# A hybrid S5, retention and SwiGLU layer on one core: S5 parameter scratch in the table memory, padded C cleared at the start, key products and norm steps placed later or earlier

## The chip, the cores and the metric

The kernel runs on one core of a Trainium2 chip. The metric is the device time of one execution in microseconds (us); lower is better. The core has a matrix engine (PE, with its weight loads shown apart as PEld), a vector engine (DVE), a scalar engine (ACT), a general engine (POOL), and SP, which here only issues DMAs. The profile's times count from the start of its span.

## The reference

The reference computes one layer for 256 prompt tokens and 8 sequences of 8 decode tokens, 320 tokens in all, at width 2048, in fp32. Cut to what matters:

```
h = rms_norm(x, norm_mix)
u, q, k, v, g = split(h @ w_in)                 # widths 1024 each
s5 = s5_mixer(u, state, lam, log_step, b, c, d, w_glu, b_glu)
o  = retention_chunked(rotary(q), rotary(k) * 128**-0.5, v, state)   # 8 heads of 128
ret = silu(g) * group_norm(o) * ret_gn_w
x = x + concat([s5, ret]) @ w_out
gate, up = split(rms_norm(x, norm_ffn) @ w_ffn_in)
x = x + (silu(gate) * up) @ w_ffn_out
y = rms_norm(x, norm_final)

# s5_mixer: 64 groups of 16 channels, 64 complex states each
lam_bar = exp(lam * dt);  b_bar = ((lam_bar - 1) / lam) * b
xs = associative_scan(a * x + b_bar @ u)        # over the tokens
y  = Re(c @ xs) + d * u;  gelu(y) * sigmoid(gelu(y) @ w_glu + b_glu)

# retention, per head and chunk of 128 tokens
scores = (q @ k.T) * mask
o = scores @ v + (q @ r) * q_decay
r = r * chunk_decay + (k * k_decay).T @ v
```

The outputs are y for all tokens, and the new S5 and retention states.

## The kernel before, in words

**Matrix products.** Each weight is read in fp32 and split into two parts, hi (a cast on ACT, L130) and lo (a difference on DVE, L131); the activations are split in the same way. A 128 x 128 piece of a weight then goes through PE in three products with all 320 tokens (L141 to L143): hi by xhi, hi by xlo, lo by xhi. These three are called a block below. The function gemm runs blocks one after the other; the projections' result is ps_p.

**What runs between the blocks.** Everything else (the S5 part and the retention heads) is written as generators. After each block gemm adds 0.4 to a counter, clk.now, and run_due starts every generator whose time has come; a generator that yields a number sleeps for that much of the counter. The numbers are in the table DL (L799). They set the order on PE and on POOL, which follow the program's order. SP's order stands in the program, too, while a scheduler orders ACT and DVE by priorities; instructions under tc.high_priority go ahead.

**S5 parameters.** Once at the start, some 100 small DVE operations turn lam and log_step into the powers of lam_bar and their products (s5_step, L359, and s5_params, L365): rr, lp, ff, gp, the cosines and sines ecs, and lx0, the start states by lam_bar^4. Their intermediates are cut out of a piece of scratch by T(), and newscr(i) sets which piece (L319). It is the memory of cls_[i], named cl in the profile: cl is the padded C matrix of an S5 chunk, 1280 columns on 128 partitions, two of them, used by chunks in turn. s5_step begins in cls_[0], the exponentials of the parameters go to cls_[1] (newscr(1)), and lx0 is worked out in cls_[0] again. When that is done, POOL clears both cl (L451), so that the chunks find zeros where C is padded.

**S5 tables.** From ecs POOL builds tab, the cosines and sines of every chunk's 64 steps: 32 columns in four groups of 8 (s5_tables, L460). Group 0 is built at once, the groups 1 to 3 later, about 68 counter units apart (L415). Chunk c's scan on DVE reads four of the columns (s5_chunk, L500), so a group serves two chunks. A chunk has transposes (pt), small products (pk_, pb), the scan, and its output product py, into which cl goes.

**Retention heads.** Three generators for each of the 8 heads:
- head_k (L642): the key transposes pst; ACT scales them into kd and copies the decode keys into kv; the scores pss by three products; DVE multiplies the scores by the mask mk into sm (two parts) and smp (decode).
- head_v (L663): the value transposes pst2 (a pst in the profile too); ACT scales them into vT; DL["o"] later the output po = sm by vT and smp by vT, then the state product psr. DVE takes statistics of po (bn_stats, bn_aggr: st, mv). POOL makes scale and shift of them in eight small steps (L696 to L703: mv, gy), ACT normalises into `on` (L706), and DL["c"] later PE transposes `on` back into pn.
- pst, pss, pst2, pt, pk_, psr, pn all share one PSUM tag, misc, with two buffers.

**Second norm.** Late in the output projection ffn_norm (L1029) sums the squares, acc, on PE into ps_r, DVE takes the reciprocal root in some 12 small steps (ms, ry, rt), and PE spreads it over the partitions (ps_r2). DL["n2"] and DL["n2b"] place the two PE steps.

Of the kernel before, what the change touches and what calls it, by code (L numbers as in the profile page):

```python
# [44 lines left out]
def hybrid_kernel(ctx, tc, xT, w_in, w_out, w_glu, w_fi, w_fo, vecs, s5p, bc, x0,  # L45
# [3 lines left out]
    pe, act, dve, pool, sp = nc.tensor, nc.scalar, nc.vector, nc.gpsimd, nc.sync  # L49
# [20 lines left out]
    o = 0  # L70
# [104 lines left out]
    def tt(out, a, b, op):  # L175
        dve.tensor_tensor(out, a, b, op)
        return out
# [118 lines left out]
    tab = s5.tile([P, 2, NPAIR, NCP], F32, name="tab", tag="tab", bufs=1)  # L296
# [14 lines left out]
    d0s = [s5.tile([P, 2, 4, NCP], F32, name=f"d0{i}") for i in range(2)]  # L311
    xps = [s5.tile([P, 2, 4, NC], F32, name=f"xp{i}") for i in range(2)]
    cls_ = [s5.tile([P, 2, 4, CH + 1, 32], F32, name=f"cl{i}") for i in range(2)]
    bl0 = s5.tile([P, 2, 2, 2, 32], F32, name="bl0")
    kbd = s5.tile([P, CH, P], F32, name="kbd")
    for t_ in (*d0s, *xps, bl0, kbd):
        pool.memset(t_, 0.0)
    scr = [None, 0]

    def newscr(i):  # L320
        scr[0] = cls_[i].rearrange("p r j t h -> p (r j t h)")
        scr[1] = 0

    def T(shape):
# [34 lines left out]
    def s5_params(dt_):  # L359

        ang = T(she)
        tt(ang[:, 0], prm[:, 1], dt_, MUL)
        ts(ang[:, 1], ang[:, 0], 8.0, MUL)
        ts(ang[:, 2], ang[:, 0], 64.0, MUL)
        nn = ts(T(she), ang, float(1 / np.pi), MUL, MAGIC, ADD)  # L365
        ts(nn, nn, MAGIC, SUB)
        for part in PI_PARTS:
            stt(ang, nn, -part, ang, MUL, ADD)
        par = ts(T(she), nn, 0.5, MUL, MAGIC, ADD)
        ts(par, par, MAGIC, SUB)  # L370
        stt(par, nn, 0.5, par, MUL, SUB)
        tt(par, par, par, MUL)
        ts(par, par, -8.0, MUL, 1.0, ADD)
        a2 = tt(T(she), ang, ang, MUL)
        ec, es = ecs[:, 0:NE], ecs[:, NE:]
        q = T(she)
        ts(q, a2, 1.0 / factorial(13), MUL, -1.0 / factorial(11), ADD)
        for kk in (9, 7, 5, 3, 1):
            tt(q, q, a2, MUL)
            ts(q, q, (1.0 if (kk // 2) % 2 == 0 else -1.0) / factorial(kk), ADD)  # L380
        tt(q, q, ang, MUL)
        tt(es[:, 0::3], q, par, MUL)
        q = T(she)
        ts(q, a2, -1.0 / factorial(14), MUL, 1.0 / factorial(12), ADD)
        for kk in (10, 8, 6, 4, 2, 0):
            tt(q, q, a2, MUL)
            ts(q, q, (1.0 if (kk // 2) % 2 == 0 else -1.0) / factorial(kk), ADD)
        tt(ec[:, 0::3], q, par, MUL)
        for l in range(2):
            n = (NE - 1 - l + 2) // 3  # L390
            c_, s_ = ec[:, l::3][:, :n], es[:, l::3][:, :n]
            u1, u2 = T([P, n, NPAIR]), T([P, n, NPAIR])
            tt(u1, c_, c_, MUL)
            tt(u2, s_, s_, MUL)
            tt(ec[:, l + 1::3][:, :n], u1, u2, SUB)
            stt(es[:, l + 1::3][:, :n], c_, 2.0, s_, MUL, MUL)
        for g in range(4):
            if g == 0:
                for _ in s5_tables(ec, es, g):
                    pass  # L400
            else:
                spawn(s5_tables(ec, es, g), max(0.0, T0 - 40.0 + 2 * PER * g - clk.now))
        newscr(1)
        lr = tt(T(sh), prm[:, 0], dt_, MUL)
        vexp(rr, lr, sh)
        tt(lp[:, 0, 0], rr, ec[:, 0], MUL)
        tt(lp[:, 1, 0], rr, es[:, 0], MUL)
        den = tt(T(sh), prm[:, 0], prm[:, 0], MUL)
        d2 = tt(T(sh), prm[:, 1], prm[:, 1], MUL)
        tt(den, den, d2, ADD)  # L410
        rden = T(sh)
        dve.reciprocal(rden, den)
        nr = ts(T(sh), lp[:, 0, 0], -1.0, ADD)
        t1 = tt(T(sh), nr, prm[:, 0], MUL)
        t2 = tt(T(sh), lp[:, 1, 0], prm[:, 1], MUL)  # L415
        tt(t1, t1, t2, ADD)
        tt(ff[:, 0], t1, rden, MUL)
        t3 = tt(T(sh), lp[:, 1, 0], prm[:, 0], MUL)
        t4 = tt(T(sh), nr, prm[:, 1], MUL)
        tt(t3, t3, t4, SUB)  # L420
        tt(ff[:, 1], t3, rden, MUL)
        r2 = tt(T(sh), rr, rr, MUL)
        tt(r4, r2, r2, MUL)

        def cmul(o, a, b, shape):

            u1, u2 = T(shape), T(shape)
            tt(u1, a[0], b[0], MUL)
            tt(u2, a[1], b[1], MUL)
            tt(o[0], u1, u2, SUB)  # L430
            tt(u1, a[0], b[1], MUL)
            tt(u2, a[1], b[0], MUL)
            tt(o[1], u1, u2, ADD)

        def ri(t, i):
            return (t[:, 0, i], t[:, 1, i])

        def rep_(t, n):
            return tuple(t[:, q].unsqueeze(1).to_broadcast([P, n, NPAIR]) for q in range(2))

        cmul(ri(lp, 1), ri(lp, 0), ri(lp, 0), sh)
        cmul(ri(lp, slice(2, 4)), rep_(lp[:, :, 1], 2), ri(lp, slice(0, 2)), [P, 2, NPAIR])
        cmul(ri(gp, slice(0, 3)), rep_(ff, 3), ri(lp, slice(0, 3)), [P, 3, NPAIR])
        newscr(0)

        def b8(a):
            return a.unsqueeze(2).to_broadcast(shx)

        cmul((lx0[:, 0], lx0[:, 1]), (x0t[:, 0], x0t[:, 1]), (b8(lp[:, 0, 3]), b8(lp[:, 1, 3])), shx)
        for t_ in cls_:  # L450
            pool.memset(t_, 0.0)  # L451
        for q in range(2):
            for d in range(2):
                o = lpc[:, :, q, 4 * d:4 * d + 4]
                act.mul(o, lp[:, q].rearrange("p e (c j) -> p c j e", j=4), -1.0 if d > q else 1.0)
                o = gpc[:, :, q, 4 * d:4 * d + 4]
                act.copy(o[:, :, :, 0], ff[:, q].rearrange("p (c j) -> p c j", j=4))
                act.copy(o[:, :, :, 1:], gp[:, q].rearrange("p e (c j) -> p c j e", j=4))
# [41 lines left out]
    def s5_chunk(c):  # L500
# [21 lines left out]
        for w_, pc in ((0, gpc), (1, lpc)):  # L522
# [14 lines left out]
            for g in range(2):  # L537
                ps_, hs = slice(64 * g, 64 * g + 64), slice(16 * g, 16 * g + 16)
                if w_:
                    tt(cl[ps_, 0, :, 1:, hs], m1[ps_, 0:4], m2[ps_, 4:8], SUB)  # L540
                    tt(cl[ps_, 1, :, 1:, hs], m1[ps_, 4:8], m2[ps_, 0:4], SUB)
        yield DL["b1"] + (4.0 if c == 0 else 0.0)
        bst = s5.tile([P, 8, P], F32, name="bst", tag="bst", bufs=1)[:, 0:4]
# [3 lines left out]
        act.copy(bst, pt.rearrange("p (i s) -> p i s", s=P))  # L547
        yield DL["k1"]
        pk_ = misc("pk_")
# [5 lines left out]
        for j in range(4):  # L555
            r = slice(32 * j, 32 * j + 32)
            act.copy(kbd[r, :, r], pk_[r, 0:P].rearrange("p (d h) -> p d h", h=32))
        yield DL["b2"]
        pb = ps_b.tile([P, 2, 512], F32, name="pb", tag="pb", bufs=1)
# [32 lines left out]
        for r in range(2):  # L592
            act.copy(xs[:, r, :, :, 0], x0t[:, r, js])
            act.copy(xs[:, r, :, :, 1], ends[:, 0, r, js])
        yield DL["scan"]
        py = ps_y.tile([P, 512], F32, name="py", tag="y", bufs=1)
# [43 lines left out]
        return a  # L640

    def head_k(h, q_, qg, k_, R):  # L642
        yield DL["k"] + (2.5 if h == 0 else 0.0)
        pst = misc("pst")
        for i, s in enumerate(STARTS):
            tr(pst[:, P * i:P * i + P], k_[:, s:s + P])
        kd = mp.tile([P, 2, P], F32, name="kd", tag="kd", bufs=1)
        for i in range(2):
            act.mul(kd[:, i], pst[:, P * i:P * i + P], kdc[:, h, i:i + 1])
        act.mul(kv[64:128, h], pst[64:128, 2 * P:3 * P], kdc[64:128, h, 2:3])  # L650
        pss = misc("pss")
        mm(0.43, pss[:, 0:256], k_[:, 0:P], q_[:, 0:256], start=True, stop=True)
        mm(0.22, pss[:, 256:384], k_[:, P:256], q_[:, P:256], start=True, stop=True)
        mm(0.22, pss[:, 384:448], k_[:, 192:320], q_[:, 256:320], start=True, stop=True)
        sm = mp.tile([P, 384], F32, name="sm", tag="sm", bufs=1)
        mk = R["mk"]
        tt(sm[:, 0:256], pss[:, 0:256], mk[:, 0:NP], MUL)
        tt(sm[:, 256:384], pss[:, 256:384], mk[:, 0:P], MUL)
        tt(smp[64:128, :, 0:NS], pss[64:128, 384:448].rearrange("p (b t) -> p b t", t=NS),
           mk[64:128, NP:320].rearrange("p (b t) -> p b t", t=NS), MUL)  # L660
        R["kd"], R["sm"] = kd, sm

    def head_v(h, v_, qg, rt, R):  # L663
        yield DL["v"]
        pst2 = misc("pst2")
        for i, s in enumerate(STARTS):
            tr(pst2[:, P * i:P * i + P], v_[:, s:s + P])
# [27 lines left out]
        m_, t_, y_, w_ = mv[:, 0], mv[:, 1], y[:, 0], y[:, 1]  # L695
# [93 lines left out]
    def do_g(h):  # L789
        ps = proj(11 + 4 * h)  # L790
        sg = mp.tile([P, N], F32, name="sg", tag="sg", bufs=2)
        with tc.high_priority(offset=EVAC):
# [3 lines left out]
        spawn(sg_mul(h, sg))  # L796
        run_due()

    DL = dict(b1=14.2, k1=2.2, b2=4.6, scan=15.6, x=2.2, k=5.5, v=6.1,  # L799
              o=2.2, u=6.0, c=10.0, n2=3.0, n2b=2.4, nm=7.8)  # L800
    T0, PER = 52.6, 34.0


# [6 lines left out]
    with tc.high_priority(offset=100000):  # L810
        with tc.manual_schedule(engines={mybir.EngineType.SP}):
            act.dma_start(vec, vecs)
            k0 = 0
            for b, k1 in enumerate((2, 4, 8, 12, 16)):
                c, q = k0 // 4, slice(k0 % 8, (k1 - 1) % 8 + 1)
# [109 lines left out]
        tt(u2, src[1], m[0], MUL)  # L925
        tt(out[:, 1], u1, u2, ADD)

    newscr(1)
    finp = s5.tile([P, 2, NPAIR], F32, name="finp", tag="m0", bufs=1)
    fins = s5.tile([P, 2, NPAIR, NB], F32, name="fins", tag="m1", bufs=1)  # L930
    fin(finp.unsqueeze(3), [endp[:, r].unsqueeze(2) for r in range(2)],
# [301 lines left out]
```

## Time and profile before

| | |
|---|---|
| median of three runs | 1486.57 us (1485.52 to 1486.83) |
| the profiled execution | 1487.18 us |
| its span, first to last instruction | 1485.4 us |
| mean granted TensorE clock | 0.991 |
| PE busy from 57 to 92 us (35 us) | 25.83 us, granted clock 0.85 |
| PE busy from 272 to 283 us (11 us) | 6.86 us, granted clock 0.69 |
| PE busy from 545 to 1160 us (615 us) | 615.00 us, granted clock 1.00 |
| HBM read, written | 219.35 MB, 8.95 MB |

A row of a timeline gives the start, the length of the busy stretch, the engine, the line of the kernel, the operation with what it writes and reads, and, in brackets, how long the engine was idle before it and what released it. A row of the waits gives the engine, the tile and line that waited, the engine, tile and line that ended the wait, and then the sum, the number and the longest of such waits. The granted clock is the share of full speed that the throttle gave PE; the tenths in the profile's overview show it at 8 of 10 in two of forty slices and at 9 (90% or more) in the others.

### The profile page before, as it was taken

Reading aid. Unit: us, or ns where it says so; the run is one execution under the profiler, and the core shown is the slowest. Engines: PE = TensorE matmul, PEld = TensorE weight load, DVE = VectorE, ACT = ScalarE, POOL = GpSimd, SP = SyncE. Lnnn points to the kernel's source line nnn. Section 1 sums busy time; section 2 is a strip of 40 time slices with the busy share of each in tenths; the row PEclk is TensorE's granted clock in tenths of the full one; section 3 lists DMA queues with packets and bytes.
Section 4 is the critical chain, followed back from the end, with each engine's and each line's share of the span. In section 5 each row is a group of like instructions: output and inputs, shape, how many; then the busy total and the mean of one; then the engine's idle time right before and its main releaser. Section 6 shows DMA issues by size and latency. Waiting matters only on the chain.

```text
span 1485.4 us, 26187 instructions
## 1 busy us (share of the span) xinstructions
PE 1450.8 (98%) x10654; PEld 1430.6 (96%) x10654; DVE 849.8 (57%) x1411; ACT 616.5 (42%) x988; POOL 104.1 (7%) x228
## 2 busy tenths in 40 slices
PE   8979999899999999999999999999999999999997
PEld 7979999899999999999999999999999999999996
DVE  8967667567846765665445444444444454444454
ACT  6545555554525543333333333333333333333352
POOL 1333501412000000000000000000000000000001
PEclk9989999999999999999999999999999999999998
DMA  7534444344644466665444345444444544445443
GB/s 268 160 112 146 139 148 147 111 137 127 207 146 152 146 213 191 214 216 185 155 145 155 119 154 168 157 150 148 139 137 152 172 153 147 152 123 152 148 150 110
DMA packets 82312, 232.10 MB, mean 156 GB/s; under 512 B 17808, under 2 KB 30224, under 8 KB 82192
## 3 DMA queue, kind: packets, MB, share of 16 engines
q1 hardware_dynamic: 82048, 230.39, 48.9%
q8 instruction: 84, 1.38, 0.4%
q14 instruction: 36, 0.29, 0.1%
q10 hardware_dynamic: 144, 0.04, 0.0%
HBM read 219.35 MB, written 8.95 MB: 154 GB/s over the span
## 4 chain that ended last, share of the span: by engine, by line
PE 68%; DVE 1%; DMA 0%; ACT 0%; issue 0%; DVEq 0%; SPq 0%
PE ps_fo L142 7%; PE ps_fu L143 7%; PE ps_fo L143 7%; PE ps_fu L141 7%; PE ps_fu L142 7%; PE ps_fo L141 7%; PE ps_fg L143 7%; PE ps_fg L141 7%; PE ps_fg L142 7%; PE ps_o L141 1%; PE ps_o L142 1%; PE ps_o L143 1%; PE ps_g L142 1%; PE ps_g L143 1%; PE ps_g L141 1%; DMA raw<-w_fi 0%
## 5 line engine op out<-in xcount | busy, mean ns | idle before, releaser
L131 DVE TENSOR_TENSOR lo<-raw,hi 128x1024 fp32r<-128x1024 f32 (+1 forms) x420 | 472.2, 1125 | 419.0 <-ACT hi L130 417.8
L130 ACT CAST hi<-raw 128x1024 fp32r<-128x1024 f32 (+1 forms) x420 | 406.8, 969 | 685.5 <-PE ps_fo L142 189.1
L141 PE MATMUL ps_fg<-hhi,hi 128*128 128x320 f32 x704 | 217.6, 309 | 0.0
L143 PE MATMUL ps_fo<-ahi,lo 128*128 128x320 f32 x704 | 217.5, 309 | 0.0
L142 PE MATMUL ps_fo<-alo,hi 128*128 128x320 f32 x704 | 217.5, 309 | 0.0
L141 PE MATMUL ps_fo<-ahi,hi 128*128 128x320 f32 x704 | 217.5, 309 | 0.0
L143 PE MATMUL ps_fg<-hhi,lo 128*128 128x320 f32 x704 | 217.4, 309 | 0.0
L143 PE MATMUL ps_fu<-hhi,lo 128*128 128x320 f32 x704 | 217.4, 309 | 0.0
L142 PE MATMUL ps_fg<-hlo,hi 128*128 128x320 f32 x704 | 217.4, 309 | 0.0
L142 PE MATMUL ps_fu<-hlo,hi 128*128 128x320 f32 x704 | 217.4, 309 | 0.0
L141 PE MATMUL ps_fu<-hhi,hi 128*128 128x320 f32 x704 | 217.4, 309 | 0.0
L141 PE MATMUL ps_p<-xhi,hi 128*128 128x320 f32 x576 | 184.7, 321 | 0.0
L143 PE MATMUL ps_p<-xhi,lo 128*128 128x320 f32 x576 | 179.2, 311 | 0.0
L142 PE MATMUL ps_p<-xlo,hi 128*128 128x320 f32 x576 | 179.1, 311 | 0.0
L142 PEld LDWEIGHTS ps_fg<-hlo,hi 128*128 128x128 f32 x704 | 132.4, 188 | 0.3
L141 PEld LDWEIGHTS ps_fg<-hhi,hi 128*128 128x128 f32 x704 | 132.3, 188 | 0.3
L143 PEld LDWEIGHTS ps_fu<-hhi,lo 128*128 128x128 f32 x704 | 132.4, 188 | 0.0
L141 PEld LDWEIGHTS ps_fu<-hhi,hi 128*128 128x128 f32 x704 | 132.4, 188 | 0.0
L142 PEld LDWEIGHTS ps_fu<-hlo,hi 128*128 128x128 f32 x704 | 132.4, 188 | 0.0
L143 PEld LDWEIGHTS ps_fg<-hhi,lo 128*128 128x128 f32 x704 | 132.3, 188 | 0.0
L141 PEld LDWEIGHTS ps_fo<-ahi,hi 128*128 128x128 f32 x704 | 132.1, 188 | 0.0
L142 PEld LDWEIGHTS ps_fo<-alo,hi 128*128 128x128 f32 x704 | 132.1, 188 | 0.0
(419 smaller groups left out, 1976.9 us busy)
## 6 DMA issues: line engine op xcount, KB each, us to landing
raw<-w_fi SPq DMA_DIRECT2D x176, 512.0 KB
raw<-w_in SPq DMA_DIRECT2D x76, 512.0 KB
raw<-w_fo SPq DMA_DIRECT2D x64, 512.0 KB
raw<-w_out SPq DMA_DIRECT2D x32, 512.0 KB
raw<-w_fo SPq DMA_DIRECT2D x64, 192.0 KB
rt<-r SPq DMA_DIRECT2D x8, 512.0 KB
raw<-w_glu SPq DMA_DIRECT2D x8, 512.0 KB
raw<-r SPq DMA_DIRECT2D x8, 512.0 KB
```

Of the source, the lines that this page charges most:

```text
L130: act.copy(hi[:, :m], raw[:, :m])
L131: dve.tensor_tensor(lo[:, :m], raw[:, :m], f(hi[:, :m]), SUB)
L141: pe.matmul(ps, hi, xhi[:, k], start=k == 0, stop=False)
L142: pe.matmul(ps, hi, xlo[:, k], start=False, stop=False)
L143: pe.matmul(ps, lo, xhi[:, k], start=False, stop=k == nk - 1)
```

## The change

It has three parts.

1. **Clear.** The two cl are cleared by POOL at the kernel's start with the other tiles that begin as zeros, and no longer in s5_params.
2. **Scratch.** The parameters' scratch no longer lies in cl but in tab: newscr(0) and newscr(1) give columns 15 to 31 of the cosine and the sine half (17 x 64 = 1088 columns each). Column 15 is the last of table group 1, the others are groups 2 and 3, all of which POOL builds later. The final states' scratch, used after the last chunk, is cls_[1] as before, now called newscr(2).
3. **Placing.** All key products come later (DL["k"] from 5.5 to 8.5); head 0 loses its own extra of 2.5 there, so that it moves by 0.5, and its value products get an extra of 3.0. The second norm's sums come earlier (n2 from 3.0 to 2.4), and the spread a little later behind them (n2b from 2.4 to 2.6).

```diff
-    for t_ in (*d0s, *xps, bl0, kbd):
+    for t_ in (*d0s, *xps, bl0, kbd, *cls_):
         pool.memset(t_, 0.0)
     scr = [None, 0]
 
     def newscr(i):
-        scr[0] = cls_[i].rearrange("p r j t h -> p (r j t h)")
+
+        scr[0] = (tab[:, i, 15:].rearrange("p j t -> p (j t)") if i < 2 else
+                  cls_[1].rearrange("p r j t h -> p (r j t h)"))
         scr[1] = 0
...
         cmul((lx0[:, 0], lx0[:, 1]), (x0t[:, 0], x0t[:, 1]), (b8(lp[:, 0, 3]), b8(lp[:, 1, 3])), shx)
-        for t_ in cls_:
-            pool.memset(t_, 0.0)
...
     def head_k(h, q_, qg, k_, R):
-        yield DL["k"] + (2.5 if h == 0 else 0.0)
+        yield DL["k"]
...
     def head_v(h, v_, qg, rt, R):
-        yield DL["v"]
+        yield DL["v"] + (3.0 if h == 0 else 0.0)
...
     DL = dict(b1=14.2, k1=2.2, b2=4.6, scan=15.6, x=2.2, k=5.5, v=6.1,
-              o=2.2, u=6.0, c=10.0, n2=3.0, n2b=2.4, nm=7.8)
+    DL = dict(b1=14.2, k1=2.2, b2=4.6, scan=15.6, x=2.2, k=8.5, v=6.1,
+              o=2.2, u=6.0, c=10.0, n2=2.4, n2b=2.6, nm=7.8)
...
-    newscr(1)
+    newscr(2)
     finp = s5.tile([P, 2, NPAIR], F32, name="finp", tag="m0", bufs=1)
```

How the numbers move the groups on PE, in blocks since the start of the kernel (before / after):

| head | key transposes and scores | value transposes | po | pn |
|---|---|---|---|---|
| 0 | 100 / 102 | 96 / 102 | 100 / 108 | 126 / 133 |
| 1 | 156 / 164 | 174 / 171 | 180 / 177 | 201 / 199 |
| 2 | 238 / 246 | 255 / 253 | 260 / 259 | 283 / 279 |
| 3 | 318 / 322 | 333 / 326 | 338 / 332 | 361 / 354 |
| 4 | 394 / 399 | 415 / 415 | 419 / 419 | 444 / 444 |
| 5 | 455 / 463 | 479 / 479 | 483 / 483 | 509 / 509 |
| 6 | 519 / 527 | 543 / 543 | 547 / 547 | 573 / 573 |
| 7 | 573 / 577 | 589 / 582 | 594 / 588 | 617 / 610 |

The second norm's sums move from block 968 to 967, the spread from 975 to 974. The S5 transposes pt stay at 146, 265, 399, 463 and 527, and at heads 2, 3 and 7 move from 201 to 205, 334 to 332 and 591 to 588.

POOL's row at the end of the first table group, before (tab, ta and tabl are the table and its temporaries, cl_136 and cl_137 the two padded C, mv and gy the statistics of head 0 and what becomes of them):

```order
L482 TENSOR_TENSOR tab<-tab,ta 128x8x32
L486 COPY tabl<-tab 128x2x8
L451 MEMSET cl_136 128x1280
L451 MEMSET cl_137 128x1280
L696 TENSOR_SCALAR mv<-mv 128x4
L697 TENSOR_SCALAR mv<-mv 128x4
L698 TENSOR_TENSOR gy<-mv,mhalf 128x4
```

And in the changed kernel:

```order
L482 TENSOR_TENSOR tab<-tab,ta 128x8x32
L486 COPY tabl<-tab 128x2x8
L696 TENSOR_SCALAR mv<-mv 128x4
L697 TENSOR_SCALAR mv<-mv 128x4
L698 TENSOR_TENSOR gy<-mv,mhalf 128x4
L699 TENSOR_TENSOR gy<-gy 128x4
```

The two clears between the table and head 0's statistics are gone from here; they stand with the clears at the kernel's start.

DVE's row around the scores of head 0, before (cl_137 is the scratch, rr, lp, ff and r_122 are parameters, pss the scores, sm and smp the masked scores):

```order
L176 TENSOR_TENSOR cl_137<-cl_137 128x32
L176 TENSOR_TENSOR sm<-pss,mk 128x256
L170 TENSOR_SCALAR cl_137<-cl_137 128x32
L176 TENSOR_TENSOR sm<-pss,mk 128x128
L176 TENSOR_TENSOR rr<-cl_137 128x32
L176 TENSOR_TENSOR smp<-pss,mk 64x8x8
L176 TENSOR_TENSOR lp<-rr,ecs 128x32 x2
L176 TENSOR_TENSOR cl_137<-rr 128x32
L170 TENSOR_SCALAR cl_137<-lp 128x32
L176 TENSOR_TENSOR cl_137<-lp,prm 128x32 x2
L176 TENSOR_TENSOR cl_137<-cl_137,prm 128x32 x2
L176 TENSOR_TENSOR r_122<-cl_137 128x32
```

And in the changed kernel, where the scratch is called tab:

```order
L176 TENSOR_TENSOR tab<-lp 128x32
L176 TENSOR_TENSOR ff<-tab 128x32 x2
L176 TENSOR_TENSOR tab<-lp 128x32
L176 TENSOR_TENSOR sm<-pss,mk 128x256
L176 TENSOR_TENSOR lp<-tab 128x32
L176 TENSOR_TENSOR sm<-pss,mk 128x128
L176 TENSOR_TENSOR tab<-lp 128x32 x2
L176 TENSOR_TENSOR tab<-lp 128x64
L131 TENSOR_TENSOR lo<-raw,hi 128x1024
L176 TENSOR_TENSOR lp<-tab 128x32
L176 TENSOR_TENSOR smp<-pss,mk 64x8x8
L176 TENSOR_TENSOR tab<-lp 128x64
```

The masked scores stand behind ff now, and a difference of a weight (lo) and more of the parameters lie between their parts.

PE's row around the key products of head 5, before (py is an S5 chunk's output product, ps_p the projection):

```order
L142 MATMUL ps_p<-xlo,hi 128x320
L143 MATMUL ps_p<-xhi,lo 128x320
L102 MATMUL py<-xp_134,cl_136 32x80 x32
L107 MATMUL pst<-ident,k__3493 128x128 x3
L102 MATMUL pss<-q__3354,k__3493 128x256
L102 MATMUL pss<-q__3354,k__3493 128x128
L102 MATMUL pss<-q__3354,k__3493 128x64
L141 MATMUL ps_p<-xhi,hi 128x320
```

And in the changed kernel, where pt are the S5 transposes of the next chunk:

```order
L141 MATMUL ps_p<-xhi,hi 128x320
L142 MATMUL ps_p<-xlo,hi 128x320
L143 MATMUL ps_p<-xhi,lo 128x320
L107 MATMUL pst<-ident,k__3493 128x128 x3
L102 MATMUL pss<-q__3354,k__3493 128x256
L102 MATMUL pss<-q__3354,k__3493 128x128
L102 MATMUL pss<-q__3354,k__3493 128x64
L107 MATMUL pt<-ident,bl 128x128 x4
L141 MATMUL ps_p<-xhi,hi 128x320
```

The key products stood right behind py; now eight blocks lie between, and the S5 transposes follow the scores at once.

More of the change, by code (lines that the diff above doesn't have):

```diff
@@ L797, in do_g @@
         run_due()
-    DL = dict(b1=14.2, k1=2.2, b2=4.6, scan=15.6, x=2.2, k=5.5, v=6.1,
-              o=2.2, u=6.0, c=10.0, n2=3.0, n2b=2.4, nm=7.8)
+    DL = dict(b1=14.2, k1=2.2, b2=4.6, scan=15.6, x=2.2, k=8.5, v=6.1,
+              o=2.2, u=6.0, c=10.0, n2=2.4, n2b=2.6, nm=7.8)
     T0, PER = 52.6, 34.0
```

## The prediction

> **What bounds the kernel now.** I read the page's engine shares and its chain first, then the waits of PE, then the granted clock around the two longest waits, and last the timelines there.
>
> ```profile
> span 1485.4 us, 26187 instructions
> PE 1450.8 (98%) x10654; PEld 1430.6 (96%) x10654; DVE 849.8 (57%) x1411; ACT 616.5 (42%) x988; POOL 104.1 (7%) x228
> PE 68%; DVE 1%; DMA 0%; ACT 0%; issue 0%; DVEq 0%; SPq 0%
> ```
>
> PE is busy 98% of the span and the chain that ended last is PE. No other engine can shorten the run except by ending one of PE's idle times, and these are 34.6 us in all (1485.4 less 1450.8). The waits of PE say which of them the change can reach (tile, line, what it waited for; sum, times, longest):
>
> ```profile
> PE pn L107 <- ACT on L706: 7.9, 1, 7.9
> PE pst L107 <- DVE k__3493 L176: 4.1, 1, 4.1
> PE pst L107 <- DVE k__3974 L176: 1.9, 1, 1.9
> PE ps_r L102 <- DVE ry L180: 1.5, 1, 1.5
> PE po L102 <- DVE sm L176: 1.2, 1, 1.2
> PE pst L107 <- DVE k__4354 L176: 1.2, 1, 1.2
> PE pst L107 <- DVE k__2360 L176: 0.7, 1, 0.7
> ```
>
> That is 18.5 us in seven places: head 0's normalised output (pn) and its scores (po), the key products of heads 3, 5, 6 and 7 (pst), and the second norm (ps_r). A wait also costs something afterwards. The next view gives stretches of about 3.3 us: length, PE's busy time, the granted clock, DMA.
>
> ```profile
> 74.00:77.20 3.20, 0.21 (x2) 1.00 0.50 166
> 80.80:84.00 3.20, 1.86 (x7) 0.50 0.08 25
> 84.20:87.40 3.20, 3.20 (x13) 0.50 0.02 5
> 87.60:91.00 3.40, 3.40 (x25) 1.00 0.51 154
> 272.00:275.20 3.20, 0.89 (x52) 1.00 0.02 9
> 275.40:278.60 3.20, 1.57 (x6) 0.50 0.45 164
> 278.80:282.00 3.20, 3.20 (x14) 0.50 0.14 36
> 316.40:319.60 3.20, 1.34 (x34) 1.00 0.37 82
> ```
>
> Both long waits leave PE at half clock, until about 87.5 and 282.1 us. The 1.9 us wait at 317 us does not, though PE worked only 1.34 of those 3.2 us.
>
> **Head 0: the clear that POOL no longer does here.** Start, length, engine, line, operation:
>
> ```profile
> 53.36 1.23 POOL L472 COPY tab<-ecs 128x8 f32<-128x8 f32 x1 [48.28 <-DVE ecs L176]
> 64.89 0.17 DVE L693 BATCH_NORM_AGGREGATE mv<-st 128x2 f32<-128x6 f32 x1
> 75.25 2.27 POOL L451 MEMSET cl<- 128x1280 f32 x2 [6.44 <-DVE lx L176]
> 77.49 0.33 POOL L696 TENSOR_SCALAR mv<-mv 128x4 f32<-128x4 f32 x1
> 81.39 0.20 POOL L703 TENSOR_TENSOR gy<-mv,gy 128x4 f32<-128x4 f32 x1
> 81.63 1.50 ACT L706 ACTIVATE on<-po,gy 128x128 f32<-128x128 f32 x4 [2.94 <-POOL gy L703]
> 82.14 1.52 PE L107 MATMUL pn<-ident,on 128*128 128x128 f32 x4 [7.93 <-ACT on L706]
> 88.38 0.31 PE L141 MATMUL ps_p<-xhi,hi 128*128 128x320 f32 x1
> 88.82 0.31 PE L141 MATMUL ps_p<-xhi,hi 128*128 128x320 f32 x1
> ```
>
> The statistics were ready at 65.06, but POOL stood until 75.2 at a clear of cl that had to wait for DVE's last reading of the scratch in it (for lx). The eight small steps behind it (77.49 to 81.59) then held ACT, and ACT held PE. With the scratch in the table memory the two clears stand at the kernel's start, ahead of 48 us in which POOL only waits for ecs (53.36); I cost the 2.3 us there at nothing (uncovered they would be 2.3). The wait of 7.9 us goes, and half clock from 82.14 to 87.5 with it, worth 5.4/2 = 2.7 us.
>
> What is late next is the score product. The change puts head 0's key products 2 blocks later and its po group 8 blocks later, and the vector engine's row now has sm and smp behind more of the parameters. Its rows before:
>
> ```profile
> 55.37 0.49 PE L107 MATMUL pst<-ident,v__778 128*128 128x128 f32 x3
> 57.94 0.23 DVE L176 TENSOR_TENSOR cl<-cl 128x32 f32<-128x32 f32 x1
> 59.54 0.41 DVE L176 TENSOR_TENSOR sm<-pss,mk 128x256 f32<-128x256 f32 x1
> 63.00 0.49 DVE L176 TENSOR_TENSOR ff<-cl 128x32 f32<-128x32 f32 x2
> 65.58 0.97 DVE L176 TENSOR_TENSOR cl<-lp 128x32 f32<-128x32 f32 x3
> 68.99 1.21 DVE L131 TENSOR_TENSOR lo<-raw,hi 128x1024 fp32r<-128x1024 f32 x1
> ```
>
> From 57.94 to the end of ff at 63.49 the parameters take 5.55 us, 0.8 of it sm's three parts. Without these, ff ends at 62.7. Then come, by their own lengths before, one lp product (0.35), sm (0.34), an lp row (0.58), sm's second part (0.2), three products (1.16), a lo of 1.14 and an lp row (0.2); smp (0.26) ends at about 66.9. PE is there earlier: it had the value products at 55.37; without them there, 6 blocks of 0.44 us (88.38 to 88.82) later it starts the key products at 58.0, the value products follow at 59.6 behind the eviction of the keys (0.5 us, below), and after 6 more blocks it reaches po at 62.5. It waits for sm until 63.4, for the second part until 64.2, for smp until 66.9. What is queued behind on DVE (lo, the chunk's bl and cl) is late by no more than before, since the same work is in front; PE is the one who waits.
>
> Then po, its short products and psr take 1.8 us (before: 60.84 to 62.6), 25 blocks 11.0 us, pn 0.6: PE is through with pn at 80.3. Is `on` there? The statistics start behind the next DVE rows at 69.6 and end at 71.1, POOL's steps take 4.1, `on` 1.5: 76.7, while pn is reached at 79.7. pn stands 7 blocks later than before, so the block behind it is before's eighth behind pn, which began at 88.4 after seven blocks mostly at half clock. So head 0 gives 8.1 us, if the clock holds.
>
> It probably doesn't: a stretch of 3.4 us within 62.5 to 66.9 has only some 0.7 us of work, less than the 0.89 after which the clock was halved at 275 us. The two halvings above lasted some 10.2 and 6.8 us; the difference, 3.4, is the shortest that I can infer, 1.7 us lost; the others lost 2.5 and 2.7 behind their wait. I take 1.9, nearest to the shortest, because PE works without a gap from 66.9. Ends: 0 and 3. **Head 0: -8.1 + 1.9 = -6.2 us.** The Trainium skill, "TensorE: Matmul & The Clock Gate", Part 1 and the table in "Why this matters for your kernels", holds that the clock is kept as long as no idle gap between bursts exceeds about 3 us. By that rule the gaps here (0.9, 0.3 and 2.7 us) leave the clock full and the sum is 1.9 us better; the row at 272 to 275 us, halved after some 2.3 us of idling, speaks against it.
>
> **Heads 3, 5, 6, 7: key products later.**
>
> ```profile
> 236.75 0.55 PE L107 MATMUL pst<-ident,k__2970 128*128 128x128 f32 x3
> 237.93 0.39 PE L141 MATMUL ps_p<-xhi,hi 128*128 128x320 f32 x1
> 237.97 0.37 ACT L650 ACTIVATE kv<-pst,kdc 64x128 f32<-64x128 f32 x1
> ```
>
> Head 5's products stand 8 blocks later, 3.5 us, against a wait of 4.14: 0.6 stays. Its half clock (277.03 to 282.1) goes, 5.07/2 = 2.5. So -3.5 - 2.5 = -6.0. Heads 3 (4 blocks and an S5 product), 6 (8 blocks) and 7 (4 blocks and an S5 product) move by more than they waited: -0.7 - 1.9 - 1.2 = -3.8.
>
> What it adds: at heads 4, 5 and 6 the S5 transposes pt now follow the key products at once, and with two PSUM buffers pt needs the one that ACT's kd and kv read. PE is through with the products 1.18 us after they start (236.75 to 237.93), ACT at 238.34: pt waits 0.4 and a little, 0.45 each, **+1.3 us** (ends 0.9, and 4.5 if a weight cast of 1.05 us stands in front each time). Head 1 has 13 blocks instead of 24 between its scores and po, and vT behind the scan's last copy on ACT: +0.3 (0 to 1). The later scores of the other heads keep 10 blocks (4.4 us) or more.
>
> **Second norm.** Both steps come one block earlier.
>
> ```profile
> 536.30 0.49 DVE L176 TENSOR_TENSOR acc<-acc,sqx 128x320 f32<-128x320 f32 x1
> 537.85 0.16 DVE L172 TENSOR_SCALAR ms<-ps_r 128x3 f32<-128x3 f32 x1 [1.06 <-PE ps_r L102]
> 541.11 1.23 DVE L131 TENSOR_TENSOR lo<-raw,hi 128x1024 fp32r<-128x1024 f32 x1
> 542.26 0.15 DVE L180 SCALAR_TENSOR_TENSOR ry<-rt,ry 128x3 f32<-128x3 f32 x1
> ```
>
> The sums at 536.65 wait 0.2 us for acc. In the changed row the lo at 541.11 stands behind ry instead of in front, so ry ends 1.15 earlier, at about 541.1, and PE, there at 540.8, waits 0.3: 0.5 in place of 1.5, **-1.0 us** (ends 0 and -1.5).
>
> **Sum.** -6.2 - 6.0 - 3.8 + 1.3 + 0.3 - 1.0 = -15.4 us. The profiled execution took 1487.18 us (1.8 around its span), so it gives 1471.8; the median of the runs is 0.6 lower, so the forecast is **1471.2 us**, 1.0% faster. The rest, from 640 blocks on, is weights through PE without waits, and begins that much earlier.
>
> **Rivals.**
> - The clock stays full at head 0: 1471.2 - 1.9 = 1469.3. For it the row at 316 us; against it, less work in the stretch. Chance 0.15.
> - DVE bounds head 0 harder: its parameter rows share the time with POOL's table steps, and another 3 us on smp, with a second half-clock stretch and casts in front of pt, take 6 back: 1477.2. Chance 0.12.
> - The change doesn't free POOL: if the table's first clears for the second group, which wait for the same lx, held the statistics as cl's clear did, the stall at pn would stay and 6.2 be lost: 1477.4. The new row has the statistics in front. Chance 0.06.
> - Slower: scores reach po too late at heads 1 to 7. At 4.4 us of room, a delay from pss to smp of 7 us at all seven costs 2.6 each, 18.2: 1489.4. It decides from about 2.6 us a head; the DVE order keeps sm where it was, which speaks against it. Chance 0.04.
>
> **Numbers.** The forecast has 0.60, 0.03 is left for a gain lost in waits that I don't see. Faster by over 0.2% (about what a measurement of this kernel can tell from no change) 0.93, within 0.03, slower 0.04. Best bounds (no halving, no pt waits, sm 1.5 earlier) reach 1466.5, the two cases that lose 6 us end at 1477.4, and a little of both 1478.5.
>
> **What would show it.** pn should be gone from PE's waits, POOL's clears should stand before 8 us, and `on` should end before 78. A wait at po for sm and smp of 3 to 4.5 us should be the longest left after 50 us, with half clock for 3.4 us behind it; without the halving the sum is 1.9 better. No wait over 1 us at a pst, three of about 0.45 at pt, full clock at 275 us; ps_r about 0.5. Wrong: a stall at pn still, or po waits at heads 1 to 7.

## The result, and the profile after

| | before | changed |
|---|---|---|
| median, first comparison | 1486.57 us (1485.52 to 1486.83) | 1472.84 us (1471.69 to 1475.28) |
| ratio, 95% interval | | 0.9911 (0.9894 to 0.9928) |
| median, second comparison | 1485.95 us (1485.67 to 1489.78) | 1474.35 us (1473.81 to 1476.22) |
| ratio, 95% interval | | 0.9920 (0.9905 to 0.9935) |
| profiled execution, first comparison | 1487.18 us | 1473.51 us |

The change is 0.8 to 0.9% faster, 11.6 to 13.7 us. The forecast was 1471.2 us.

The page and the waits of PE in the changed kernel (waiting engine, tile and line, what it waited for; sum, times, longest):

```profile
span 1471.7 us, 26212 instructions
PE 1448.6 (98%) x10654; PEld 1428.9 (97%) x10654; DVE 851.5 (58%) x1411; ACT 614.3 (42%) x988; POOL 106.7 (7%) x228
...
PE psu L1067 <- issue: 2.7, 1, 2.7
PE po L102 <- DVE smp L176: 2.0, 1, 2.0
PE po L102 <- DVE lp L176: 0.9, 1, 0.9
PE pt L107 <- ACT kv L650: 0.8, 3, 0.3
PE pst L107 <- DVE k__3493 L176: 0.4, 1, 0.4
PE ps_r L102 <- DVE ry L180: 0.3, 1, 0.3
```

The wait at pn is gone, head 5's has shrunk from 4.1 to 0.4, and those of heads 3, 6 and 7 are no longer listed. Two waits took their place: the one at po that the prediction named, and one at psu, the products that update the retention states during the feed-forward part, that it did not. The waits in the kernel's first 25 us, where the inputs are loaded, are left out here: at 34.6 us both executions start the same product (ps_r, 34.56 and 34.59), so up to there the clears at the start cost nothing.

Head 0 in the changed kernel, in order of time (start, length, engine, line, operation):

```profile
4.91 2.27 POOL L317 MEMSET cl<- 128x1280 f32 x2
63.69 0.91 PE L102 MATMUL po<-vT,sm 128*128 128x128 f32 x6 [0.88 <-DVE lp L176]
66.23 0.23 DVE L176 TENSOR_TENSOR smp<-pss,mk 64x64 f32<-64x64 f32 x1
66.61 1.19 PE L102 MATMUL po<-vT,smp 128*128 128x128 f32 x4 [2.01 <-DVE smp L176]
71.23 0.17 DVE L693 BATCH_NORM_AGGREGATE mv<-st 128x2 f32<-128x6 f32 x1
71.50 0.32 POOL L696 TENSOR_SCALAR mv<-mv 128x4 f32<-128x4 f32 x1 [1.40 <-DVE mv L693]
77.09 1.50 ACT L706 ACTIVATE on<-po,gy 128x128 f32<-128x128 f32 x4 [4.00 <-POOL gy L703]
80.83 0.60 PE L107 MATMUL pn<-ident,on 128*128 128x128 f32 x4
```

The clears end at 7.2 us, POOL begins with the statistics 0.1 us after they are ready (71.40), and `on` is there 2.2 us before PE reaches pn. The stretches around po (length, PE's busy time, granted clock, DMA):

```profile
63.00:66.40 3.40, 0.91 (x6) 1.00 0.03 7
66.40:69.80 3.40, 3.19 (x25) 0.51 0.45 159
```

One stretch of half clock follows the waits, from 66.5 to 69.9 us, of the length that was inferred.

How far the two executions are apart is read from products that both have. PE's rows of before:

```profile
94.11 0.60 PE L107 MATMUL pt<-ident,bl 128*128 128x128 f32 x4
451.32 0.41 PE L142 MATMUL ps_g<-ylo,hi 128*128 128x320 f32 x1 [0.34 <-DVE ylo L180]
542.47 0.93 PE L102 MATMUL ps_r<-ident,ry 128*128 128x128 f32 x6 [1.47 <-DVE ry L180]
607.50 0.63 PE L1067 MATMUL psu<-lo,hi 128*128 128x512 f32 x2
```

And of the changed kernel:

```profile
86.98 0.60 PE L107 MATMUL pt<-ident,bl 128*128 128x128 f32 x4
435.50 0.42 PE L142 MATMUL ps_g<-ylo,hi 128*128 128x320 f32 x1 [0.34 <-DVE ylo L180]
525.41 0.93 PE L102 MATMUL ps_r<-ident,ry 128*128 128x128 f32 x6 [0.32 <-DVE ry L180]
593.86 0.62 PE L1067 MATMUL psu<-lo,hi 128*128 128x512 f32 x2
```

Row by row the lead of the changed kernel is 7.1 behind head 0 (block 146), 15.8 behind the heads, 17.1 at the second norm's spread (of which 0.4 is the block by which it moved), and then 13.6 behind the first state updates; the two executions end 13.7 apart. So some 3 us are lost between the second norm and 594 us. The timeline of the changed kernel there:

```profile
571.62 0.68 DVE L176 TENSOR_TENSOR hi<-lo,bmk 128x512 fp32r<-128x512 f32 x1
576.95 0.68 DVE L180 SCALAR_TENSOR_TENSOR raw<-raw,psu 128x512 f32<-128x512 f32 x1
577.54 1.22 DVE L131 TENSOR_TENSOR lo<-raw,hi 128x1024 fp32r<-128x1024 f32 x1
578.68 0.68 DVE L176 TENSOR_TENSOR hi<-lo,bmk 128x512 fp32r<-128x512 f32 x1
579.47 0.48 PE L1067 MATMUL psu<-hi 128*128 128x512 f32 x1 [2.73 <-issue]
```

And of before:

```profile
586.89 0.69 DVE L176 TENSOR_TENSOR hi<-lo,bmk 128x512 fp32r<-128x512 f32 x1 [0.27 <-DMA lo<-hi]
591.76 0.68 DVE L176 TENSOR_TENSOR hi<-lo,bmk 128x512 fp32r<-128x512 f32 x1
592.96 0.62 PE L1067 MATMUL psu<-hi 128*128 128x512 f32 x2
```

`hi<-lo,bmk` is the second operand of the state update, in two halves. Before, both halves are done ahead of the first psu product. In the changed row of DVE the second half stands behind the reader of the first psu product (raw<-raw,psu) and a weight difference (lo), and the second psu product begins 0.1 us after it ends (579.36). The view names no releaser ("issue"), but these rows fit DVE's order; whether it is the cause was tried below.

### The profile page after: what moved, and what is told of

Same layout as the page of the kernel before. It is cut to its first block, busy times and chain, and to the rows that moved or that the text cites. A ratio compares the mean times of both kernels' runs of the same rounds, so it can differ in the third digit from the quotient of the medians.

```text
span 1471.7 us, 26212 instructions
## 1 busy us (share of the span) xinstructions
PE 1448.6 (98%) x10654; PEld 1428.9 (97%) x10654; DVE 851.5 (58%) x1411; ACT 614.3 (42%) x988; POOL 106.7 (7%) x228
## 4 chain that ended last, share of the span: by engine, by line
PE 69%; DVE 0%; DMA 0%; issue 0%; ACT 0%; DVEq 0%; SPq 0%
PE ps_fu L142 7%; PE ps_fo L142 7%; PE ps_fo L143 7%; PE ps_fu L143 7%; PE ps_fu L141 7%; PE ps_fo L141 7%; PE ps_fg L143 7%; PE ps_fg L142 7%; PE ps_fg L141 7%; PE ps_o L141 1%; PE ps_o L142 1%; PE ps_o L143 1%; PE ps_g L142 1%; PE ps_g L143 1%; PE ps_g L141 1%; DMA raw<-w_fi 0%
## 5 line engine op out<-in xcount | busy, mean ns | idle before, releaser
L143 PEld LDWEIGHTS ps_fo<-ahi,lo 128*128 128x128 f32 x704 | 132.1, 188 | 0.0
```

Of the source, the lines that this page charges most:

```text
L143: pe.matmul(ps, lo, xhi[:, k], start=False, stop=k == nk - 1)
```

## The experiments

Each was timed in alternation with the kernel before, whose median in the three series was 1486.05, 1485.95 and 1486.83 us.

### The clears and the scratch alone

```diff
-        yield DL["k"]
+        yield DL["k"] + (2.5 if h == 0 else 0.0)
...
-        yield DL["v"] + (3.0 if h == 0 else 0.0)
+        yield DL["v"]
...
-    ... k=8.5 ... n2=2.4, n2b=2.6
+    ... k=5.5 ... n2=3.0, n2b=2.4
```

> Only the scratch and the clears are moved; all delays are those of the kernel before. Theory (the clear of cl on POOL, which waits for DVE's last reading of the scratch, is what held head 0's output): POOL's steps start when the first table group ends, at about 68.8 us, take 4 to 5.5, the normalising 1.5, so `on` is there at 74.4 to 75.8 against PE's arrival at 74.2: the wait at pn falls from 7.9 to 0.2-1.6 us, and the half clock behind it (2.7) goes: 9 to 10.4 us gained, 1476.2 to 1477.5 us. The waits of heads 3, 5, 6, 7 (0.7, 4.1, 1.9, 1.2) stay. Rival (the placing does it, the clear was covered): within 1 us of before, 1486.6.

Measured: 1478.88 us (1477.81 to 1482.27), ratio 0.9954 (0.9942 to 0.9967). Of its waits of PE:

```profile
PE pst L107 <- DVE k__3974 L176: 1.8, 1, 1.8
PE ps_p L141 <- DVE q__1084 L176: 0.8, 1, 0.8
PE ps_p L143 <- DVE lo L131: 0.7, 1, 0.7
```

And two of its stretches, around head 6's key products (length, PE's busy time, granted clock, DMA):

```profile
305.70:309.10 3.40, 1.55 (x67) 1.00 0.21 49
309.10:312.50 3.40, 3.40 (x15) 0.51 0.33 125
```

No wait at pn is left, with the delays of before: the clear on POOL was the stall, and the rival falls. The gain of 7.2 us is 2 to 3 us short of what was expected: PE, coming earlier, now waits 1.5 us for a weight difference and for head 1's q, and head 6's wait of 1.8 us, which cost no clock before, is followed by half clock here.

### The placing alone

```diff
-    for t_ in (*d0s, *xps, bl0, kbd, *cls_):
+    for t_ in (*d0s, *xps, bl0, kbd):
...
+        for t_ in cls_:
+            pool.memset(t_, 0.0)
```

(and the scratch in cl again.)

> Only the delays are changed; scratch and clears stand where they stood before. Theory: the clears wait for DVE's last lx (about 75.9 us here), 2.3 us of clears, 4 to 5.5 of POOL's steps and 1.5 of normalising bring `on` at 83.7 to 85.2; PE reaches pn at about 80.8, so pn waits 2.9 to 4.4 us more than with both parts, with one to two stretches of half clock (1.7 to 2.7 us) behind it: 4.5 to 7 us slower than the full change, 1477.3 to 1480. Heads 5, 6, 7 wait no more than in the full change. The second product of the state update (psu) waits some 2.7 us, as in the full change. Rival (the placing does it all): 1472.8.

Measured: 1479.21 us (1478.56 to 1480.29), ratio 0.9954 (0.9941 to 0.9968). Of its waits of PE:

```profile
PE pn L107 <- ACT on L706: 4.6, 1, 4.6
PE psu L1067 <- issue: 2.7, 1, 2.7
```

And POOL in its timeline:

```profile
76.01 2.28 POOL L451 MEMSET cl<- 128x1280 f32 x2 [5.83 <-DVE lx L176]
```

As expected: the clear waits for lx, pn for POOL (4.6 us, a little more than expected), and psu waits as in the full change. Alone, the two parts gain 7.2 and 6.8 us, 14.0 in sum, against 11.6 to 13.7 for both. That the sum comes so near does not make them independent: both shorten the same wait at pn (the placing alone from 7.9 to 4.6), and the clears alone pay short waits and a half-clock stretch at 309 us that the change's profile does not have.

### Head 0's masked scores ahead of the parameters on DVE

```diff
-        tt(sm[:, 0:256], pss[:, 0:256], mk[:, 0:NP], MUL)
...
+        with tc.high_priority(offset=GN if h == 0 else 0):
+            tt(sm[:, 0:256], pss[:, 0:256], mk[:, 0:NP], MUL)
...
```

> The full change, with head 0's three masked-score products ahead of the parameters on DVE. Theory (the waits at po are DVE's order, and the half clock follows from them): the waits for sm (0.9) and smp (2.0) go, and with them the half clock at 66.5 to 69.9 us (1.7): 4.5 us gained, 1468.3 us. Rival (the halving there does not depend on the waits, or the later parameters hold the first chunk): 2.9 or less gained, 1470 to 1472.8. The wait at the state update stays at 2.7 us.

Measured: 1472.26 us (1471.22 to 1472.84), ratio 0.9906 (0.9893 to 0.9920). Of its waits of PE:

```profile
PE psu L1068 <- issue: 2.7, 1, 2.7
PE ps_p L143 <- DVE lo L131: 0.7, 1, 0.7
PE pn L107 <- ACT on L707: 0.4, 1, 0.4
```

And its stretches around the wait at psu:

```profile
574.10:577.50 3.40, 0.67 (x4) 1.00 0.43 143
577.50:580.90 3.40, 3.40 (x15) 0.51 0.76 288
```

Both waits at po are gone, so they were DVE's order, and the half clock behind them is gone with them. The gain of 4.5 us did not come: 1.5 us return as short waits (pn, lo, and 0.2 each for q and for retp), the first pt is 2.2 us earlier than in the change, measured from the first ps_r of each, and in this execution the wait at psu is followed by half clock, as it was not in the change's first profile.

### Head 0 back at its old place

```diff
-        yield DL["k"]
+        yield DL["k"] - (0.5 if h == 0 else 0.0)
...
-        yield DL["v"] + (3.0 if h == 0 else 0.0)
+        yield DL["v"]
```

> The full change, but head 0's three groups stand where they stood before (keys at block 100, values at 96). Theory: no wait for smp and no half clock; the wait for sm is 1.2 us as before, pn waits 0.2 to 1.6. The block behind pn's seventh neighbour then starts at about 79 us, where the full change has it at 81.2: 1.5 to 3 us gained, 1470 to 1471.3 us. Rival (head 0 had to go later, since pn waits again for POOL): a wait at pn of 3 us or more with half clock behind it, 1474 or more.

Measured: 1473.50 us (1472.62 to 1475.48), ratio 0.9917 (0.9904 to 0.9931).

pn waits for nothing, so the rival falls: with the clears away, head 0 needs no later place. But here, too, PE pays for its earliness with the same two waits as with the clears alone (0.8 us for head 1's q, 0.7 for lo). In this execution the wait of 2.7 us at psu is also followed by half clock, from 576.7 to 580.2 us, which the change's first profile did not have. So the time expected was not reached, and head 0's new place neither gains nor loses what these runs can tell.

### The change once more, and the norm at its old place

```diff
-              o=2.2, u=6.0, c=10.0, n2=2.4, n2b=2.6, nm=7.8)
+              o=2.2, u=6.0, c=10.0, n2=3.0, n2b=2.4, nm=7.8)
```

> The changed kernel once more, as a base for the others on the same chip. Theory (the wait of 2.7 us at psu is set by the order of DVE's instructions): it is there again, between 2.6 and 2.8 us, in another execution. Whether the clock is halved behind it and behind head 0's po depends on where the waits fall among the 3.41 us stretches, which begin at another time in every execution: 1471 to 1475.5 us. Rival (the wait at psu was a late DMA of that one execution): no wait over 1 us at psu, 1470 to 1471.5.

> The full change with the second norm's two steps where they stood before. DVE's row then has both halves of the state operand ahead of the first reader of psu again. Theory: the wait at psu goes (2.7 us, and 1.7 more in the executions in which the clock was halved behind it), the wait at ps_r goes back from 0.3 to 1.5: 1.5 to 3.2 us faster than the full change. Rival (the stall at psu has nothing to do with DVE's order): 1.2 us slower than the full change.

Measured: the change 1474.35 us (above), the old norm 1472.07 us (1470.10 to 1474.51), ratio 0.9903 (0.9886 to 0.9920). The change's second profile has the wait of 2.7 us at psu again; its stretches there:

```profile
575.30:578.70 3.40, 1.29 (x9) 1.00 0.47 159
578.70:582.10 3.40, 2.77 (x10) 0.50 0.54 159
582.10:585.50 3.40, 3.40 (x15) 0.50 0.38 154
```

The profile with the old norm has no wait at psu, and this one, with half clock behind it:

```profile
PE ps_r L102 <- DVE ry L180: 2.1, 1, 2.1
```

The wait of 2.7 us at psu is there in every kernel whose DVE row has the second half behind the reader (the change twice, the placing alone, the masks first, head 0 back, and the filled wait below), and there is no wait at psu in those whose row has both halves ahead of the first psu product (before, the clears alone, the old norm). So it is not a late DMA of one execution. The two intervals overlap, so the times alone do not settle that the old norm is better, but the norm's step did not pay: what it took at ps_r it lost at psu.

### Head 0's wait filled with products

```diff
+        if h == 0:
+            for _ in range(11):
+                pe.matmul(po[:, 2], ident, ident, start=True, stop=True)
```

> The full change, with 11 products of 128 x 128 by the identity (some 1.8 us) put into head 0's wait for smp; what they write into po is overwritten. Theory (PE's idling halves the clock): the wait for smp falls from 2.0 to about 0.2, and the clock stays full from 60 to 90 us: 1.3 us faster than the full change up to the first pt, 0.5 to 1.5 in the median. Rival (the halving there comes from elsewhere): half clock from about 66 to 70 us as before, 0 to 0.5 us slower.

Measured: 1475.96 us (1474.33 to 1476.26), ratio 0.9926 (0.9911 to 0.9941). Its stretches around po:

```profile
63.00:66.40 3.40, 3.02 (x27) 1.00 0.04 7
66.40:69.80 3.40, 3.40 (x39) 1.00 0.83 247
```

The half clock is gone from here, as the theory has it, but this one execution does not show that the products did it: with the placing alone, PE waited 0.4 and 2.4 us at the same two places, unfilled, and the clock stayed full. There an edge of the clock's stretches, at 65.4 us, fell into the longer wait, so that PE was busy 1.9 and 2.1 us of the two stretches (see the last section). The time did not improve: DVE's row has head 0's statistics later, at 72.6 and no longer 70.1; pn waits 0.8 us behind them, another 0.8 go into a wait for a weight difference, and half clock follows psu from 581.0 to 584.4 us. As a time this run shows nothing of the clock.

### Masks first, and the norm between

```diff
-              o=2.2, u=6.0, c=10.0, n2=2.4, n2b=2.6, nm=7.8)
+              o=2.2, u=6.0, c=10.0, n2=2.6, n2b=2.2, nm=7.8)
```

(together with the masks' priority above.)

> Masked scores of head 0 first, and the norm's delays 2.6 and 2.2, so that the sums stand at block 967 as in the change, the spread at 973, and both halves of the state operand ahead of the reader of psu. Theory: from 1472.3 with the masks alone the 2.7 us at psu go, and the 1.7 of half clock that its profile shows behind it; the wait at ps_r rises by 0.4: 2.3 to 4 us faster than the masks alone, 1468.3 to 1470. Rival: the norm waits for the sums of squares, or psu for the copies of the states, and 1 us or less is gained.

Measured: 1469.81 us (1469.49 to 1470.14), ratio 0.9886 (0.9870 to 0.9903). The second half of the state operand and the second psu product in its timeline:

```profile
575.28 0.68 DVE L176 TENSOR_TENSOR hi<-lo,bmk 128x512 fp32r<-128x512 f32 x1
576.06 0.48 PE L1068 MATMUL psu<-hi 128*128 128x512 f32 x1 [1.00 <-PE psu L1068]
```

This is the lowest median, 4.5 us under the change in the same series, and its range lies below the change's. The sums stand at the change's block and the spread one earlier, but the second half is ahead of psu's reader (which starts at 577.41): the 2.7 us go with DVE's order, not with the place of the sums. A wait of 1.0 us is left at psu. The view names PE itself for it, but the second product begins 0.1 us after the second half ends (575.96), as in the change. So this looks like the rest of the same wait, shorter by the reader and the weight difference that no longer stand in front. At ps_r it waits 0.7.

### What is left at head 0

> Masks first and norm at 2.6 and 2.2, with the start states' product lx0 left out (it is zero; six products of 128 x 256 and some 2.3 us of DVE less between 70 and 77 us). Theory (what is left at head 0, 0.4 at pn, 0.7 for lo, 0.2 for q and 0.2 for pn's reader, comes from `on` waiting on ACT for POOL's eight steps, with the weight casts queued behind it): pn still waits 0.4 or more, and the time is within 0.7 us of 1469.8. Rival (DVE's load is the bound there): the waits go, 1.4 us faster, 1468.4.

> Masks first and norm at 2.6 and 2.2, with the four POOL steps that refine the reciprocal root left out for head 0 alone (2.05 us of the 4.3 that its steps take). Theory: `on` starts 2 us earlier, the waits at pn (0.4) and for lo (0.7) go: 1.1 us faster, 1468.7, 1468.3 to 1469.1. Rival (DVE's load): within 0.3 us of 1469.8, the wait for lo stays.

```diff
-        cmul((lx0[:, 0], lx0[:, 1]), (x0t[:, 0], x0t[:, 1]), (b8(lp[:, 0, 3]), b8(lp[:, 1, 3])), shx)
...
-        pool.tensor_tensor(w_, y_, y_, MUL)
+        if h:
+            pool.tensor_tensor(w_, y_, y_, MUL)
...
```

(the first piece in the one, the second, four steps long, in the other; without lx0 the start states are missing from the S5 result, so that kernel serves for its time alone.) Measured: 1470.03 us (1469.22 to 1470.37) without lx0, 1470.04 us (1469.42 to 1470.68) with the short chain on POOL; 1469.81 with both whole. DVE's load is not what binds there: with 2.3 us of it gone pn still waits 0.4 and the time stays. The shorter chain removed the wait at pn, but not the loss. ACT in the timeline of the short chain:

```profile
73.32 0.46 ACT L708 ACTIVATE on<-po,gy 128x128 f32<-128x128 f32 x1 [1.61 <-POOL gy L705]
73.67 1.03 ACT L130 CAST hi<-raw 128x1024 fp32r<-128x1024 f32 x1
```

And PE:

```profile
74.76 0.41 PE L141 MATMUL ps_p<-xhi,hi 128*128 128x320 f32 x1 [1.00 <-ACT hi L130]
```

A weight cast stands right behind the first piece of `on` in ACT's row, `on` waits for POOL, and PE waits 1.0 us for the cast and then 0.7 for lo. That fits the theory's mechanism, but its 1.1 us did not come: the wait moved from pn to the cast, and in this execution half clock follows, from 76.0 to 79.4 us, which the run before it (masks first, and the norm between) did not have. Whether these last 1.5 us can be had by another order on ACT was not tried.

## Why the prediction held, and where it did not

| step | forecast | profiled executions |
|---|---|---|
| head 0 | -6.2 | -7.1 |
| heads 1 to 7 and pt | -6.0 - 3.8 + 1.3 + 0.3 = -8.2 | -8.7 |
| second norm | -1.0 | -0.8 |
| state update | 0 | +3.0 |
| sum | -15.4 | -13.6 |

- **Head 0.** Right in mechanism, wait for wait: pn gone, 0.9 at po for sm (forecast 0.9), 2.0 for smp (2.7), one half-clock stretch of 3.4 us (3.4). The size was a little off: smp ended at 66.5 and not at 66.9, and the second part of sm did not hold PE. POOL's eight steps took 5.6 us and not 4.1 (one product on 128 x 4 took 2.4 us; in the change's second profile it took 0.8 and the eight 4.6), so that `on` ended at 78.6 and not before 78; there were 2.2 us to spare. The waits at po came to 2.9 us where 3 to 4.5 were forecast, and the longest single wait behind 50 us was at psu.
- **The clock.** The rule of about 3 us of the Trainium skill ("TensorE: Matmul & The Clock Gate", "Why this matters for your kernels") would have left the clock full. The rows at 66.4 us have it halved after waits of 0.9 and 2.0 us. The measurement decides, and against that rule here.
- **Heads 1 to 7 and pt.** Right. The wait at head 5 fell from 4.1 to 0.4 (forecast 0.6), and no half clock follows it. pt waited 0.27 three times, not 0.45, and at head 1 nothing new waits.
- **Second norm.** Right as a wait: 0.3 at ps_r, as forecast.
- **The step that failed** is the sentence that the rest, from 640 blocks on, is weights through PE without waits; its term in the sum was nothing. The scheduler's order on DVE changed some 50 us behind the norm, and the second half of the state operand fell behind psu's reader. That cost 2.7 us of waiting in every profile of this order, and none, one or two stretches of half clock behind it. Without these 3 us the profiled execution would have taken 1470.5 where the sum says 1471.8. That the time came so near the forecast is in part luck: head 0 and the heads gave 1.4 us more than forecast, which hid about half of the 3.0, and no half clock followed psu in the first profile. In the second one two stretches did, and it took 1476.22 us.
- **The rivals.** The clock did not stay full at head 0; pn did not wait for POOL again; no po of heads 1 to 7 waited. The rival in which DVE holds head 0 harder did not happen, and the runs show for its neighbourhood that short waits for ACT and DVE do come back when PE gets earlier still (for example 1.5 us with head 0 at its old place).

## What to carry to other kernels

A clear, or any write that must wait for a reader, belongs where its engine has nothing to do, not in front of a chain that another engine waits for; the scratch's last reader decides, so the scratch goes where its memory is needed last. When delays are changed in a kernel whose scheduler orders some engines, the whole order of those engines is to be compared, not only the places that were edited: here edits of 0.6 and 0.2 in the second norm's delays let one DVE instruction fall behind another product's reader 50 us later, and that cost 3.0 us where the norm's step had gained 0.8.

## What the runs showed of the hardware

The half clock comes in stretches of 3.41 us, or two or three of them, wherever it was measured away from the first 25 us and from the end of the span: one at 66.5 to 69.9 us in the change and at 268.2 to 271.6 and 309.1 to 312.6 with the clears alone, two at 82.5 to 89.3 with the placing alone, three at 77.3 to 87.5 in the kernel before. Within one execution their edges lie on one grid: the two stretches with the clears alone begin 40.96 us apart, which is twelve times 3.413. The same wait of 2.73 us at psu was followed by none (the change's first profile, the placing alone), one (masks first, head 0 back, the filled wait) and two of them (the change's second profile). In the change's first profile the wait lies across the edge between two such stretches, counted on from 66.47 us (in steps of 3.413, to 578.5); in the masks-first profile it lies within one that ends at 577.5. The Trainium skill, "TensorE: Matmul & The Clock Gate", Part 1, says that the gate watches a window of 3413 ns that runs freely and does not start with the kernel. These rows agree. The spread of the times fits, but does not show it: eight executions of the change lie within 4.5 us and the four of the masks and norm within 0.7, but those with the old norm, which have no wait at psu and still 2 us each at po and ps_r, lie within 4.4.

How much work a stretch needs is settled only in part. In the twelve profiles, read on these edges and away from both ends of the span, each run of half clock began behind a stretch in which PE was busy for 0.2 to 1.7 us, and none began behind one with 1.9 or more. From 1.55 to 1.72 us both happened: PE was busy 1.57 us in the stretch before the halving at 309.1 with the clears alone and 1.72 before the one at 76.0 with the short chain, but 1.55 us at 316.2 to 319.7 in the kernel before and 1.67 at 575.1 to 578.5 in the change, after which the clock stayed full. So the busy time alone does not decide it.
